# A quarter of a copy in HBM moved from the sync and scalar queues to GpSimd's

## The chip, the cores and the metric

One core of one Trainium2 chip; the metric is the time of one execution on the device, in microseconds, as the median of several executions. The executions that are compared here are of the fast state; one run, the copy within SBUF, also had a slow one, and it is named there. The result was taken on one chip; the experiments ran on two others. Before took 822.3 us on the first and 811.3 to 811.7 us on the others, so every experiment is compared with the runs of before on its own chip.

## The reference

```python
def setup_inputs():
    return {"x": np.random.randn(8192, 8192).astype(np.float32)}

def reference(x):
    return np.fft.ifftshift(x)
```

With both sides even, `ifftshift` swaps the four quadrants crosswise. It is a copy of 268.44 MB with nothing to compute.

## The kernel before

Rows of a quadrant are 4096 floats, 16 KB. A transfer takes every eighth row of one column half: 512 rows, 8 MB. There are 32 such transfers, from HBM to HBM. Those that write the top half of `out` are issued by the sync engine, those that write the bottom half by the scalar engine.

```python
    # STEP = 8, R = C = 8192, hr = hc = 4096
    dims = [[STEP * C, hr // STEP], [1, hc]]
    for c in range(STEP):
        for col in (0, hc):
            for eng, r0, h in ((nc.sync, 0, col), (nc.scalar, hr, hc - col)):
                eng.dma_start(
                    out=bass.AP(out.tensor, out.offset + (r0 + c) * C + h, dims),
                    in_=bass.AP(x.tensor, x.offset + (hr - r0 + c) * C + hc - h, dims),
                )
```

Of the kernel before, what the change touches and what calls it, by code (L numbers as in the profile page):

```python
# [1 line left out]

# [4 lines left out]


STEP = 8  # L10


@with_exitstack
def kernel(
    ctx: ExitStack,
    tc: tile.TileContext,
    x: bass.AP,
    out: bass.AP,
):



    nc = tc.nc

    R, C = x.shape
    hr = R // 2
    hc = C // 2

    dims = [[STEP * C, hr // STEP], [1, hc]]
    for c in range(STEP):  # L30
        for col in (0, hc):
            for eng, r0, h in ((nc.sync, 0, col), (nc.scalar, hr, hc - col)):
                eng.dma_start(
                    out=bass.AP(out.tensor, out.offset + (r0 + c) * C + h, dims),
                    in_=bass.AP(x.tensor, x.offset + (hr - r0 + c) * C + hc - h, dims),
                )


# [1 line left out]
_INS = ['x']  # L40
_OUTS = [((8192, 8192), 'float32')]


def kernel(**inputs):
    import numpy as _np
    import concourse.bacc as _bacc
    import concourse.tile as _tile
    from concourse import mybir as _mybir
    from concourse.bass_utils import run_bass_kernel_spmd as _run

    nc = _bacc.Bacc("TRN2", target_bir_lowering=False, num_devices=1)  # L51
    arrays, args = {}, []
    for name in _INS:
        a = _np.ascontiguousarray(inputs[name])
        if a.dtype.kind in "iu":
            a = a.astype(_np.int64)
        arrays[f"in_{name}_dram"] = a
        args.append(nc.dram_tensor(f"in_{name}_dram", a.shape, _mybir.dt.from_np(a.dtype), kind="ExternalInput").ap())
    for i, (shape, dtype) in enumerate(_OUTS):
        dt = _mybir.dt.from_np(_np.dtype(dtype))  # L60
        args.append(nc.dram_tensor(f"out_{i}_dram", shape, dt, kind="ExternalOutput").ap())
    with _tile.TileContext(nc) as tc:
        kernel(tc, *args)
    r = _run(nc, [arrays], core_ids=[0])
    got = tuple(r.results[0][f"out_{i}_dram"] for i in range(len(_OUTS)))
    return got[0]
```

## Time and profile before

| | before |
|---|---|
| time | 822.26 us (821.98 to 822.82, 6 runs) |
| rate of copying, 20 to 800 us | 328 GB/s |
| bytes read and written in HBM, over the span | 654 GB/s |
| sync queue / scalar queue, share of 16 engines | 50.2% / 49.7% |
| shortest / median / mean packet of 16 KB | 608 / 773 / 801 ns |

The time comes from the result, the rate from a stretch of the timeline, the next rows from the page of the profile, and the last from the trace's record of each packet (a start, a length and a queue). The copied bytes are counted once in "GB/s" and twice, read and written, in the HBM figure. The lines themselves are in the prediction.

### The profile page before, as it was taken

What the parts mean: (1) busy time and instruction counts of PE and PEld (TensorE: products, weight loads), DVE (VectorE), ACT (ScalarE), POOL (GpSimd) and SP (SyncE); (2) the same over time, 40 slices, a digit from 0 to 9 for tenths busy, and PEclk for the clock granted to TensorE, in tenths of its full rate; (3) what the DMA queues carried; (4) which work ended last, traced back from release to release, by engine and by line L of the source; (5) the groups of instructions that cost most, each with busy time, mean ns of one, the idle gap of its engine ahead of it and who ended that gap; (6) DMA issues with size and microseconds to landing.
All of it is one profiled execution on the core that took longest, in us unless ns stands there. A gap on an engine that the chain in (4) does not pass through costs nothing. (4 is left out here: it accounts for less than half of the span.)

```text
span 821.3 us, 77 instructions
## 1 busy us (share of the span) xinstructions
POOL 0.2 (0%) x4
## 2 busy tenths in 40 slices
POOL 0000000000000000000000000000000000000000
DMA  9999999999999999999999999999999999999998
GB/s 304 325 328 333 326 325 330 321 329 330 325 330 330 327 328 333 329 330 330 328 328 327 334 325 330 326 326 328 331 329 330 326 332 326 328 324 333 326 328 298
DMA packets 16896, 268.44 MB, mean 327 GB/s; under 512 B 512, under 2 KB 512, under 8 KB 512
## 3 DMA queue, kind: packets, MB, share of 16 engines
q1 hardware_dynamic: 8448, 134.22, 50.2%
q10 hardware_dynamic: 8448, 134.22, 49.7%
HBM read 268.44 MB, written 268.44 MB: 654 GB/s over the span
## 5 line engine op out<-in xcount | busy, mean ns | idle before, releaser
L51 POOL MEMSET const-bfloat16-1.0<- 128x1 bf16 x1 | 0.1, 103 | 0.0
L51 POOL MEMSET const-uint8-127<- 128x1 uint8 x1 | 0.1, 102 | 0.0
L51 POOL MEMSET const-float32-0.0<- 128x1 f32 x1 | 0.1, 99 | 0.2 <-issue 0.2
L51 POOL MEMSET const-float32-1.0<- 128x1 f32 x1 | 0.1, 99 | 0.0
## 6 DMA issues: line engine op xcount, KB each, us to landing
out_dram<-in_x_dram ACTq DMA_DIRECT2D x16, 8192.0 KB, 204.3
out_dram<-in_x_dram SPq DMA_DIRECT2D x16, 8192.0 KB, 204.1
```

Of the source, the lines that this page charges most:

```text
L51: nc = _bacc.Bacc("TRN2", target_bir_lowering=False, num_devices=1)
```

## The change

The intent is to have a third queue carry a quarter of the rows from the beginning, in the hope that three queues together move more than two. Of every eight neighbouring rows, numbers 6 and 7, counted from 0, go to GpSimd, whose queue the profile calls `software_dynamic`; 0 to 5 stay with sync and scalar, whose queues it calls `hardware_dynamic`.

```diff
-    for c in range(STEP):
+
+    def copy(eng, r0, c, h):
+        eng.dma_start(
+            out=bass.AP(out.tensor, out.offset + (r0 + c) * C + h, dims),
+            in_=bass.AP(x.tensor, x.offset + (hr - r0 + c) * C + hc - h, dims),
+        )
+
+    for c in range(6):
         for col in (0, hc):
-            for eng, r0, h in ((nc.sync, 0, col), (nc.scalar, hr, hc - col)):
-                eng.dma_start(
-                    ... (the same two lines as in copy)
-                )
+            copy(nc.sync, 0, c, col)
+            copy(nc.scalar, hr, c, hc - col)
+        if c < 2:
+            for col in (0, hc):
+                copy(nc.gpsimd, 0, 6 + c, hc - col)
+                copy(nc.gpsimd, hr, 6 + c, col)
```

More of the change, by code (lines that the diff above doesn't have):

```diff
@@ L29 @@
     dims = [[STEP * C, hr // STEP], [1, hc]]
-    for c in range(STEP):
-        for col in (0, hc):
-            for eng, r0, h in ((nc.sync, 0, col), (nc.scalar, hr, hc - col)):
-                eng.dma_start(
-                    out=bass.AP(out.tensor, out.offset + (r0 + c) * C + h, dims),
-                    in_=bass.AP(x.tensor, x.offset + (hr - r0 + c) * C + hc - h, dims),
-                )
+    def copy(eng, r0, c, h):
[4 more added lines that the diff above has]
+    for c in range(6):
+        for col in (0, hc):
+            copy(nc.sync, 0, c, col)
[4 more added lines that the diff above has]
+                copy(nc.gpsimd, hr, 6 + c, col)
 _INS = ['x']
```

## The prediction

> **What bounds the kernel now.** I read the page first: the engines, the slices, the queues, and last the chain. No engine computes anything; the only busy time is 0.2 us of GpSimd's constants. The kernel is a copy from HBM to HBM, so all that counts is what the 16 DMA engines do. From the page:
>
> ```profile
> span 821.3 us, 77 instructions
> ...
> DMA  9999999999999999999999999999999999999998
> GB/s 304 325 328 333 326 325 330 321 329 330 325 330 330 327 328 333 329 330 330 328 328 327 334 325 330 326 326 328 331 329 330 326 332 326 328 324 333 326 328 298
> ...
> q1 hardware_dynamic: 8448, 134.22, 50.2%
> q10 hardware_dynamic: 8448, 134.22, 49.7%
> HBM read 268.44 MB, written 268.44 MB: 654 GB/s over the span
> ```
>
> The DMA row is 9 or more from the first slice to the last but one: there is no idle stretch to fill. The GB/s row hardly moves, 321 to 334 between its ends. The two queues' shares add to 99.9% of sixteen engines' span: together they keep the engines occupied, and each engine works on one packet at a time. 8448 packets a queue are 16 transfers of 512 rows and 16 completion words, so a packet is one row of 16,384 bytes.
>
> Next, whether issue could hold anything up. From the sync engine's waits and the list of issues:
>
> ```profile
> SPq L62 <- DMA out_dram<-in_x_dram: 167.2, 2, 118.8
> SPq L33 <- DMA out_dram<-in_x_dram: 133.8, 12, 50.6
> ...
> out_dram<-in_x_dram ACTq DMA_DIRECT2D x16, 8192.0 KB, 204.3
> out_dram<-in_x_dram SPq DMA_DIRECT2D x16, 8192.0 KB, 204.1
> ```
>
> A transfer lands 204 us after issue, and a queue finishes one about every 51 us (821.3 / 16), so four are in flight on each queue. The 133.8 us that the sync engine waits before issuing are waits for a free place behind three transfers still to be worked off. The 167.2 us is the end of the kernel, when everything is issued and only data is moving. Issue is far ahead of the data.
>
> "DMA busy" alone does not say whether the engines or the memory behind them is the limit. The trace's packet records (a start, a duration and a queue each) do. Of the 16,384 row packets the shortest took 608 ns; about a quarter took 611 ns; the median is 773 and the mean about 800 ns. A pile-up at 611 ns is an engine's own pace with nothing in its way: 16,384 B / 611 ns = 26.8 GB/s. At that pace a kernel of 1024 rows an engine would last 1024 x 0.611 = 626 us. The other 190 us or so are waiting inside packets, for something that all engines share.
>
> Stretches of the timeline tell that it is a steady common ceiling (columns: stretch, its length, GpSimd busy, clock, DMA share, GB/s):
>
> ```profile
> 3.00:5.00 2.00, 0.00 (x0) 1.00 0.92 385
> 5.00:12.00 7.00, 0.00 (x0) 1.00 1.00 351
> 12.00:20.00 8.00, 0.00 (x0) 1.00 1.00 315
> 20.00:420.00 400.00, 0.00 (x0) 1.00 1.00 328
> 420.00:800.00 380.00, 0.00 (x0) 1.00 1.00 328
> ```
>
> 328 GB/s in both long stretches, to the last digit shown. From about 5 to 12 us the packet records show the sixteen engines marching in step, all on the sync queue's rows and then all on the scalar queue's, each packet near 755 ns; later they have drifted apart and durations scatter from 611 to over 1100 ns. The scatter does not move the total. I also sorted the stretch from 20 to 790 us by how many of the engines were on one queue at the instant: the rate is 334 GB/s when all are on the scalar queue, 325 at a half-and-half mixture, 328 when all are on the sync queue. Reads and writes in opposite halves of the matrices or all in the same: it makes under 3%. That is the mark of a bandwidth ceiling, not of two address streams getting in each other's way.
>
> **What the Trainium skill says.** Three places bear on it. "DMA: Bandwidth & Descriptors", section "Issuing engines are not separate DMA queues", says that transfers started by sync, scalar or GpSimd all run on the same 16 engines and interleave, and that issuing from several only saves the sequencers' time. The trace agrees as far as two queues can show it: each takes half of one set of engines. The same page, "SWDGE vs HWDGE vs iDMA", says that GpSimd's transfers have their descriptors written by software into rings in SBUF, and that an engine goes round-robin between its internal queues; no run here shows a GpSimd transfer yet. "HBM Reference", "Specifications (TRN2)", gives about 716 GB/s for a memory stack shared by two cores. The trace's 654 GB/s, read and written together, is 91% of that. It exceeds the 358 GB/s that the page calls effective per core, so one core alone is not held to that share. I take 654 of 716 as a ceiling nearly reached; an estimate from the page's figure of the least time is 536.9 MB / 716 GB/s = 750 us[...].
>
> **The change part by part.** The program's order shows that bytes, rows and transfer shapes stay: 32 transfers of 512 rows of 16 KB. Four of sync's 16 and four of scalar's go to GpSimd, which issues eight with no wait between them; sync and scalar keep 12 each, the last eight of each with the same kind of wait as before.
>
> - Removed: 4 issues of some 42 us each from each of the two hardware queues. They lay beside data movement and were not on the path: worth 0.
> - Moved: a quarter of the packets, 8 x 512 = 4096 rows, to a third ring. Under the ceiling a packet costs its bytes whoever issued it: 67.1 MB / 328 GB/s = 205 us before and after: 0.
> - Added at the start: GpSimd's descriptors are made in software and may come a microsecond or so later than the others' first packets (an estimate; the skill's first-byte figures differ by less). Sync and scalar fill the engines meanwhile: 0.
> - Added at the end: if the three rings take turns, GpSimd moves at a third of 328 = 109 GB/s and ends its 67.1 MB at about 614 us. By then sync and scalar have moved as much each and hold 33.6 MB each, which last 67.1 MB / 328 GB/s = 205 us more. Sum 819 us, plus some 2 us before the first packet: 821 us. GpSimd is not last, so its completion handling is hidden.
> - Gain from the order in memory: three streams instead of two, with the same stride and sizes. The sort above bounds what a mixture is worth, 325 to 334: some -1% to +2%, with no reason for a sign.
>
> Sum: 821 us, against 822.3.
>
> **The rivals.**
>
> *A. The third stream raises the ceiling.* For it: for about two microseconds at the start, when only the sync queue is on, packets take about 625 ns, which is some 420 GB/s; so the memory can at least briefly take more than 328. The first-slices rates (385, 351) carry the same hint. Against it: from 20 us on, nothing in which queue is active moves the rate. If three rings took away a quarter of the 190 us of waiting, the time would be about 775 us; a tenth would give 803.
>
> *B. Software-made packets are dearer.* If a GpSimd row were cut into smaller pieces, or its descriptor fetched from the ring late, that row would take longer. For it: the skill says the rings lie in SBUF and that two of the engines are usually slower in traces, with such rings as its best guess. Every transfer is split evenly over 16 engines, so a slow pair would end last. Against it: an engine waits on average 800 - 611 = 190 ns of each packet, so an extra 100 ns on a quarter of the packets can disappear into time that is waiting anyway. If it did not disappear, 256 GpSimd rows an engine x 100 ns = 26 us: 848 us.
>
> *C. GpSimd becomes the last.* If its ring gets a smaller turn, or only few of its transfers fit, it is alone at the end. With a fifth of the rate while three are on, it would have 67.1 - 50.3 = 16.8 MB left when the others end. At the full rate of 328 that costs nothing; at half that rate, 51 us more: about 870 us. Against it: at the end of the trace of before the scalar queue is alone for about 2 us, with packets at 666 to 743 ns, no slower than in company. One ring can drive all engines; a software ring is untested.
>
> **Range and chances.** The centre is the ceiling: 821 us. The mixture's effect of -1% to +2% in rate gives about 806 to 829, widened for a mild form of A or B on either side: 804 to 840 should hold it 8 times in 10. Faster by over 2% (below 806) needs A, for which only the first microseconds speak: 0.13. Slower by over 2% (above 839) needs B or C beyond the slack: 0.13. Within 2%: 0.74.
>
> **What would show it right or wrong.** In the changed profile there should be a third queue with 67.11 MB and some 4096 packets over the completion words, and each queue's share of the engines' time in proportion to its bytes, about a quarter for GpSimd; the three still adding to about 100%. The GB/s row should stay near 328 while three queues are on and after GpSimd's end, near 614 us. The prediction is wrong if the row steps up or down at that moment (A or B); if GpSimd's queue has many more packets than its rows, or a share well above a quarter (B); or if the last slices fall while it is alone (C). Since the kernel before is steady to 0.1%, even a shift of 1% would be real, but inside what I call the same.

## The result, and the profile after

The changed kernel took 822.45 us (821.44 to 823.29, 6 runs) against 822.26 us. The ratio is 1.0001, with a 95% interval of 0.9988 to 1.0014: the same, and to within a seventh of a per cent. Ratios here are the mean time of one kernel's fast runs over that of the other's of the same rounds, so they are not quite the ratio of the medians quoted.

From the page of the changed kernel, the slices, the queues (packets, MB, share of 16 engines' span) and the issues (count, KB each, median us to landing):

```profile
span 819.7 us, 81 instructions
...
GB/s 305 330 323 329 331 325 332 328 330 329 322 333 328 328 330 325 328 330 332 330 326 336 330 328 330 329 327 329 332 327 333 324 333 326 324 333 329 329 332 295
...
q1 hardware_dynamic: 6336, 100.66, 37.4%
q10 hardware_dynamic: 6336, 100.66, 37.0%
q0 software_dynamic: 4224, 67.11, 25.3%
HBM read 268.44 MB, written 268.44 MB: 655 GB/s over the span
...
L32 POOL DMA_DIRECT2D out_dram<-in_x_dram x8 | 5.0, 631 | 0.8 <-PEq L70 0.8
...
out_dram<-in_x_dram SPq DMA_DIRECT2D x12, 8192.0 KB, 270.1
out_dram<-in_x_dram ACTq DMA_DIRECT2D x12, 8192.0 KB, 267.6
out_dram<-in_x_dram POOLq DMA_DIRECT2D x8, 8192.0 KB, 346.7
```

The third queue is there with a quarter of the bytes and a quarter of the engines' time (25.3%), and the other two have given up just that: 50.2 to 37.4 and 49.7 to 37.0. The three add to 99.7%, where the two added to 99.9. GpSimd issued all eight in 5 us. A transfer of sync's now takes 270 us from issue to landing in place of 204, because three rings share what two shared; that costs nothing, as the last landing is what counts.

The decisive view is the rate in stretches, because GpSimd's queue runs dry on the way: by the packet records its last packet ended 614.0 us after the kernel's first, 616 us into the span. Columns: stretch, its length, GpSimd busy, clock, DMA share, GB/s.

```profile
20.00:200.00 180.00, 0.00 (x0) 1.00 1.00 329
200.00:420.00 220.00, 0.00 (x0) 1.00 1.00 329
420.00:600.00 180.00, 0.00 (x0) 1.00 1.00 329
600.00:700.00 100.00, 0.00 (x0) 1.00 1.00 329
700.00:800.00 100.00, 0.00 (x0) 1.00 1.00 330
```

Three queues until 616 us, two after, and the rate doesn't notice: 329, 329, 330. Before that, from 20 to 600 us, the records count 3886 packets of GpSimd's, 3883 of sync's and 3872 of scalar's: equal turns. GpSimd's packets averaged 810 ns, sync's 798, scalar's 790. That software makes these 2% is not shown: the shortest is 608 ns on all three queues.

### The profile page after: what moved, and what is told of

It reads as the page before. It is cut to its first block, busy times and chain, and to the rows that moved or that the text cites. A ratio compares the mean times of both kernels' runs of the same rounds, so it can differ in the third digit from the quotient of the medians.

```text
span 819.7 us, 81 instructions
## 1 busy us (share of the span) xinstructions
POOL 5.2 (1%) x12
## 3 DMA queue, kind: packets, MB, share of 16 engines
q1 hardware_dynamic: 6336, 100.66, 37.4%
q0 software_dynamic: 4224, 67.11, 25.3%
## 5 line engine op out<-in xcount | busy, mean ns | idle before, releaser
L32 POOL DMA_DIRECT2D out_dram<-in_x_dram x8 | 5.0, 631 | 0.8 <-PEq L70 0.8
```

The source lines that it names most:

```text
L32: eng.dma_start(out=bass.AP(out.tensor, out.offset + (r0 + c) * C + h, dims), in_=bass.AP(x.tensor, x.offset + (hr - r0 + c) * C + hc - h, ...
```

## The experiments

The theory: some 330 GB/s of copying is a ceiling that all engines run into together, and neither the number nor the kind of the queues matters to it. The rivals: more queues do overlap better or worse; software-made packets are dearer and the small share hid it; the ceiling depends on the order of addresses; or 800 ns is simply an engine's own pace.

**All on GpSimd.** If software packets had a cost hidden by their being a quarter, four times as many show it.

```diff
-            for eng, r0, h in ((nc.sync, 0, col), (nc.scalar, hr, hc - col)):
+            for eng, r0, h in ((nc.gpsimd, 0, col), (nc.gpsimd, hr, hc - col)):
```

> All 32 transfers on GpSimd's queue, none on sync's and scalar's. Theory (a ceiling in the memory, about 328 GB/s of copying, common to all engines; who issues does not matter): 822 us within 1%, one queue with a share near 100%, packets of 611 ns at least and about 800 on average. Rival B (software-made packets are dearer, and the slack hid it while they were a quarter): with four times as many, 840 us or more, shortest packets longer than 611 ns, or two engines that end late. Rival C (a software ring alone cannot keep the engines full): GB/s clearly under 328, 870 us or more.

812.15 us against 811.29: ratio 1.0012 (0.9995 to 1.0028). The page and GpSimd's waits:

```profile
q0 software_dynamic: 16896, 268.44, 99.5%
HBM read 268.44 MB, written 268.44 MB: 662 GB/s over the span
...
POOL out_dram L33 <- DMA out_dram<-in_x_dram: 589.0, 24, 25.6
```

One software queue fills sixteen engines to 99.5%. The shortest packet is 608 ns as on the hardware queues, and the mean 787 ns is that of the next run, with all on sync. No two engines end late: sixteen packets are still under way 0.8 us before the last one ends. GpSimd spends 589 us waiting to issue its later transfers, each until an earlier one has landed: it too is ahead of the data. Rivals B and C fall for rows of 16 KB.

**All on sync.**

```diff
-            for eng, r0, h in ((nc.sync, 0, col), (nc.scalar, hr, hc - col)):
+            for eng, r0, h in ((nc.sync, 0, col), (nc.sync, hr, hc - col)):
```

> All 32 transfers on sync's hardware queue. Theory: 822 us within 1%, as with two or three queues. Rival A in its modest form (more queues overlap better): one queue should be worse than two, 830 us or more. A second reading of the first microseconds (one queue alone ran at some 420 GB/s, so one stream is what the memory likes): clearly under 806 us.

811.31 us against 811.29: ratio 1.0001 (0.9986 to 1.0016).

```profile
q1 hardware_dynamic: 16896, 268.44, 99.5%
```

One, two or three queues are the same. This also disposes of the only thing that spoke for rival A, the fast start when only the sync queue was on. Here only the sync queue is on throughout, and the packet records show the same course: 614 to 617 ns in the second and third microsecond of data, 743 in the fifth, about 787 from 20 us on. The start is fast because it is the start, not because one queue is alone. Why the ceiling lets more through for three microseconds isn't settled.

**The order of addresses.** Neighbouring rows in a transfer in place of every eighth.

```diff
-    dims = [[STEP * C, hr // STEP], [1, hc]]
+    dims = [[C, hr // STEP], [1, hc]]
...
-   (r0 + c) * C + h          (hr - r0 + c) * C + hc - h
+   (r0 + c * hr // STEP) * C + h    (hr - r0 + c * hr // STEP) * C + hc - h
```

> The kernel before with transfers of 512 neighbouring rows instead of every eighth row: same bytes, rows, queues and engines, other order of addresses (row pitch 32 KB in place of 256 KB, engines 1 MB apart in place of 8 MB). If the ceiling is a plain bandwidth that does not care for the order: 822 us within 1%. If the ceiling depends on the pattern of addresses, and the third queue changed nothing only because it kept the pattern: a difference of over 2%, either way.

811.56 us against 811.29: ratio 1.0007 (0.9984 to 1.0030). A third order (neighbouring rows to neighbouring engines; each transfer starts at row c * hr // STEP, as in the run before) was run later as a control for the runs with 14 engines:

```diff
-    dims = [[STEP * C, hr // STEP], [1, hc]]
+    dims = [[C, 16], [16 * C, hr // STEP // 16], [1, hc]]
```

> Control for the runs with fewer engines: the same order of rows (neighbouring rows to neighbouring engines) on all 16. Theory (the ceiling does not care for the order): 811 to 812 us, as before's on this chip, within 1%. If this order itself is slower, part of the 5.7% of the run with 14 engines was its order.

813.95 us against 811.63: ratio 1.0012 (0.9978 to 1.0046). So three orders of addresses agree to 0.5% at worst. The stride of every eighth row is itself worth nothing measurable on these chips. All three orders have strides that are powers of two, 32 KB and up. The nearest thing to another is in the runs with 14 engines below, where an engine's own rows are 448 KB apart and the rate, while all fourteen work, is the same.

**Half the engines.** A slowest dimension of 8 entries is meant to put a transfer on 8 engines (rows in the order of the control above).

```diff
-    dims = [[STEP * C, hr // STEP], [1, hc]]
+    dims = [[C, 8], [8 * C, hr // STEP // 8], [1, hc]]
```

> The same copy on 8 of the 16 DMA engines (slowest dimension of 8 entries), 2048 rows an engine. Theory (packets wait for the memory, which 16 engines overload): with half the demand the packets all run near the engines' own 611 ns, 8 x 26.8 = 214 GB/s, 2048 x 0.611 = 1251 us plus some 4. Rival (800 ns is the engines' own pace for copies in HBM, with a chance spread): packets keep a mean near 800 ns, 1638 us.

1249.64 us, where the theory said 1251 plus some 4 and the rival 1638. The packets on its page, and a long stretch of the run:

```profile
DMA packets 16640, 268.44 MB, mean 215 GB/s; under 512 B 256, under 2 KB 256, under 8 KB 256
...
20.00:420.00 400.00, 0.00 (x0) 1.00 0.50 216
```

The 256 packets under 512 bytes are completion words, 8 for each of 32 transfers where before had 16, and half the engines' time is used (0.50): eight engines it is. The packets no longer scatter: mean 611.3 ns, 99.9% of them at 608 to 612. So 611 ns is what an engine by itself takes for a packet, and the other 190 ns of before are spent because sixteen run at once.

**Fourteen engines.** If the ceiling is common, 14 engines should reach it as well as 16.

```diff
+    E = 14; n = hr // STEP // E     # 36; the 8 rows over go as a transfer of their own
-    dims = [[STEP * C, hr // STEP], [1, hc]]
+    dims = [[C, E], [E * C, n], [1, hc]]      # and [[C, 8], [1, hc]] for the rest
```

> The copy of before on 14 of the 16 engines (a few left-over rows on engines 0 to 7). At their own pace they would need at most 1184 x 0.611 = 723 us. Theory (one ceiling common to all engines, which 14 still reach: 14 x 26.8 = 375 GB/s of pace against some 330): the same time as with 16, within 1.5%, and shorter packets, about 14/16 of the mean. Rival (each engine has a share of its own in the ceiling, by its port): 16/14 of the time, some 14% longer.

858.77 us, ratio 1.0574 (1.0547 to 1.0601): between the two expectations. I blamed the left-over rows, which load eight of the engines and put short transfers among the long ones, and moved them once to the start:

```diff
+    for eng, r0, h in quads:
+        copy(eng, r0, h, 0, 8, 1)             # 8 rows of each quadrant, once
+    for m in (36, 36, 36, 36, 37, 37, 37, 37):  # then only transfers of 14 x m rows
```

> 14 engines again, with the left-over rows moved once at the start, so that every engine has 1170 or so rows and no short transfer sits among the long ones. Theory (ceiling common to all engines; the 5.7% before was eight engines left alone at the end with 215 GB/s, and short transfers that took places in flight): GB/s near 332 all along, within 2.5% of before, the rest being engines that do not end together. Rival (14 engines have less of the ceiling): GB/s clearly lower from the start, 5% or more.

866.29 us, ratio 1.0679 (1.0661 to 1.0697). It got worse, so my reason was wrong. The stretches show what it is instead:

```profile
20.00:220.00 200.00, 0.00 (x0) 1.00 0.88 330
220.00:470.00 250.00, 0.00 (x0) 1.00 0.87 331
470.00:770.00 300.00, 0.00 (x0) 1.00 0.82 315
775.00:860.00 85.00, 0.00 (x0) 1.00 0.50 216
```

While all fourteen work (0.88 of sixteen is 14), the rate is 330 to 331, the same as with sixteen: the ceiling is common, and the rival's 14% is not there. But the fourteen do not share it evenly. At the end eight of them are alone for 85 us at 216 GB/s, the pace of the run with eight engines. From 475 to 775 us there are spells with only eight packets under way, some 40 us in all: the other six then have nothing in flight. The loss is in the sharing, not in the total.

The packet records carry no engine number, but they show the sharing all the same. A packet mostly starts 3 or 4 ns before an earlier one ends, and so the packets of one engine can be strung together wherever just one fits. From 20 to 220 us this gives 71 strings of 20 packets or more. In 36 of them the mean packet is 611 to 621 ns, in 35 it is 749 to 804 ns, and in none is it between. The same for the kernel before, with sixteen engines and from 20 to 800 us, gives 287 strings, all of them with a mean from 771 to 833 ns. So some of the fourteen engines run almost undisturbed and the others carry all the waiting, while sixteen engines share it. An estimate: if six ran at 611 ns and eight shared the remaining 331 - 6 x 26.8 = 170 GB/s, the eight would be at 771 ns; the slow strings average 777. The six would end their 1170 rows at 715 us and the eight at 863 us, close to the span of 862.7. (In the run the eight are alone for less than these 148 us at the end, because the six were idle before.) It is not that each eight has a limit of its own near 170, since eight alone reach 216. Why six are spared isn't shown.

**Reads alone, writes alone** (wrong results): the same rows of `x` into SBUF with three tiles in turn, or all of `out` from one tile of zeros. In outline:

```diff
-   eng.dma_start(out=<rows of out>, in_=<rows of x>)
+   eng.dma_start(out=<tile in SBUF>, in_=<rows of x>)     # reads alone, one 8 MB block out at the end
+   eng.dma_start(out=<rows of out>, in_=<tile in SBUF>)   # writes alone, in the other kernel
```

> Wrong result on purpose: x is only read, into SBUF, same rows in the same order; out gets one block of 8 MB. If the ceiling is on reads and writes of HBM together (some 655 to 662 GB/s): reads alone come up against the engines' pace first, 16 x 26.8 = 429 GB/s, 626 us and about 20 for the last block: some 650 us. If reads have a ceiling of their own at 328 to 331 GB/s: 820 us or more.

> Wrong result on purpose: out is only written, from one tile of zeros in SBUF; x is not read. If the ceiling is on reads and writes together: the engines' pace, 429 GB/s, 626 us and about 20 for the fill before: some 650 us. If writes have a ceiling of their own at 328 to 331 GB/s: 820 us or more.

654.51 us and 651.02 us, at 0.81 and 0.80 of before. The stretch from 220 to 420 us of each:

```profile
220.00:420.00 200.00, 0.00 (x0) 1.00 1.01 428
```

```profile
220.00:420.00 200.00, 0.00 (x0) 0.00 (x0) 1.00 1.01 427
```

Either direction alone runs at the engines' own pace (16 x 26.8 = 429), with packets of 611 to 622 ns nearly throughout. Neither reads nor writes are limited to 330; what meets the ceiling is both at once.

**From SBUF to SBUF** (wrong result): is the ceiling at HBM, or in something the engines share whatever they copy? In outline:

```diff
-   eng.dma_start(out=<rows of out>, in_=<rows of x>)
+   eng.dma_start(out=<one of four tiles>, in_=<one tile of zeros>)    # 64 of 4 MB
```

> Wrong result on purpose: the same 268 MB from SBUF to SBUF, HBM hardly touched. If the ceiling of some 331 GB/s of copying lies on the way to HBM or in it: the engines' own pace, about 429 GB/s, 626 us and 20 to 25 for the fill before and the last block. If it lies in the engines or in what they share for any copy (reading and writing 662 GB/s together): 811 us and more, packets of 16 KB and up slowed in the same way.

994.46 us in the fast execution (the other, 1023.12, slow): neither expectation. Its rate was 285 GB/s in a stretch from 20 to 420 us, and packets of 32 KB took 1832 ns in the median against 1213 at the least, so this path has a limit of its own, a lower one. It is no measure of the other, and where the copy's ceiling sits, in the memory or in what lies between it and the engines, stays open.

**GpSimd's rows in small pieces.** The changed kernel, with every row of GpSimd's cut into pieces of 1 KB (even pieces in one transfer, odd in another).

```diff
+        w = 256 if eng is nc.gpsimd else hc
+        for odd in range(2 if w < hc else 1):
+            d = dims if w == hc else [dims[0], [2 * w, hc // (2 * w)], [1, w]]
             eng.dma_start(... + odd * w, d)
```

> The changed kernel, but GpSimd's quarter of the rows goes in pieces of 1 KB (16 packets where there was one), so software writes 16 times as many descriptors. Theory (dearer packets on a quarter disappear in the waiting as long as an engine's own paces add to less than the total: 768 rows x 0.611 = 469 us, which leaves 340 us for 4096 pieces, 83 ns each): same time within 2% if a piece takes less than 83 ns unobstructed, as 611/16 = 38 ns and a little overhead would. Rival B: software descriptors cannot be made or fetched that fast: 840 us or more, with GpSimd's queue last.

820.09 us, ratio 1.0092 (1.0076 to 1.0109). It is within the 2% and not for the reason given. The queues, and the stretches while all three were on and after; the profiled execution was the slowest of its five, 828.45 us:

```profile
q1 hardware_dynamic: 6336, 100.66, 35.5%
q10 hardware_dynamic: 6336, 100.66, 34.4%
q0 software_dynamic: 16640, 67.11, 29.1%
```

```profile
20.00:220.00 200.00, 2.04 (x1) 1.00 1.00 333
220.00:420.00 200.00, 4.07 (x2) 1.00 1.00 333
420.00:680.00 260.00, 4.08 (x2) 1.00 1.01 332
690.00:820.00 130.00, 14.27 (x7) 1.00 0.99 308
```

While three queues were on, the rate was 333. That is a mild test of slack, since undisturbed the four packets that now make up a row take 4 x 159 = 636 ns, 25 more than one of 16 KB. What moved is the order of ending. GpSimd's 16,384 packets are of 4 KB, four pieces each; the hardware queues' are of 16 KB, and a turn goes by packets: from 20 to 220 us the records count 1836 of GpSimd's, 1807 of sync's and 1800 of scalar's. By bytes that is a share of about 4/36 = 11%, not a third. The hardware queues ended 691 us into the span with their 201.3 MB, when GpSimd had moved 27 MB (12%). Its other 40 MB came alone, at 308 GB/s, with packets of 210 ns on average where the undisturbed ones took 159: less than 333, though the engines were in full use (0.99). This is rival C, at a small size. The last stretch is also the first sign that small pieces alone don't reach the ceiling of whole rows.

**All rows in pieces of 512 bytes**, on the two queues of before: does the slack hide dearer packets when all are dearer?

```diff
-    dims = [[STEP * C, hr // STEP], [1, hc]]
+    dims = [[STEP * C, hr // STEP], [256, 16], [1, 128]]     # even pieces; odd ones from + 128
```

> The kernel before in pieces of 512 bytes, on the two hardware queues: what a dearer packet costs when all are dear. The 1 KB pieces went at 159 ns for four, 40 ns each, so 2 ns over 611/16 = 38; at the same overhead 512 bytes take 19 + 2 = 21 ns, 16 KB 680 ns, which is still under the 785 or so that the ceiling gives: theory says within 2% of before. Rival B (small packets eat the slack): if a piece takes over 25 ns, the engines' pace takes over, and the time is 1024 x 32 x that: 30 ns would make 983 us.

882.19 us, ratio 1.0886 (1.0853 to 1.0918); the theory's "within 2%" was wrong. The stretch from 20 to 220 us:

```profile
20.00:220.00 200.00, 0.00 (x0) 1.00 1.10 305
```

The median record of a piece is 27 ns, not 21, and 32 x 27 = 864 ns a row, over 1024 rows 885 us, is near the span of 880.3. It is tempting to conclude that the engines now go at their own pace. The records speak against it. They overlap by some 3.5 ns (hence a share above 1), so 27 ns isn't the time from one piece to the next. From 4 to 5 us, when every piece took 27 ns, an engine did one every 23.6 ns and the sixteen 348 GB/s; at that pace a row takes 755 ns, less than the 785 that the ceiling gives. From 20 us on it was one piece every 26.6 to 26.9 ns, at 305 to 308 GB/s. So undisturbed pieces would have fitted into the slack, and the time still rose by 8.9%: small pieces make the whole slower in another way. Whether the common ceiling is lower for them, as the 308 GB/s of GpSimd's last pieces suggest, or the making of 32 times as many pieces holds the engines up, isn't shown.

No version ran faster than the kernel before.

## Why the prediction was right

- *A ceiling common to all engines, reached already.* Shown. Eight engines wait for nothing (611 ns), fourteen have the same total as sixteen, and reads or writes alone don't meet it. The direct evidence for the change is that the rate is 329 with three queues and 329 to 330 after GpSimd's end. What the Trainium skill says in "DMA: Bandwidth & Descriptors", "Issuing engines are not separate DMA queues", holds here: one queue made 811.31 us against 811.29 for two, three made 822.45 against 822.26 on the other chip. That the ceiling is the memory's bandwidth, 654 of 716 GB/s, as the prediction takes it, is not shown: no run says where it sits.
- *It doesn't care for the order of addresses.* Argued from the sort by queue; shown by three orders within 0.5%, all with strides of powers of two. The prediction allowed -1% to +2% for it and needed none.
- *Moved: 205 us before and after.* Right: 25.3% of the engines' time of 819.7 us is 207.
- *GpSimd ends at about 614 us and is not last.* Measured 614.0 after the first packet; that the last digit fits is luck. The working supposed turns by equal packets, which held because all three queues' packets were rows of 16 KB. The run with 1 KB pieces shows that it needn't: there the packets were 4 KB, the turn a quarter, and GpSimd was last.
- *Removed issues and the start are worth nothing.* Right. GpSimd's first packet came 3.8 us after sync's and 0.6 us after scalar's, where "a microsecond or so" was forecast. The first-byte figures meant there are those of "DMA: Bandwidth & Descriptors", "Specifications": about 1 us for GpSimd's path, 0.6 for the others'. Each alone, GpSimd's first packet started at 2.7 us and sync's at 2.1: 0.6 us apart, where the page has 0.4.
- *The sum of 821 us* is a span, set beside a time of 822.3 us. The spans were 821.3 before and 819.7 to 821.5 after, so it makes no difference here.
- *Rival A* rested on the first microseconds, which are as fast with one queue for good. *Rival B* was answered with slack: 190 ns of waiting in which a dearer row disappears. The runs answer it more simply. GpSimd's rows were not dearer: at their shortest they took 608 ns like the others, and with all of them on GpSimd the ratio was 1.0012. In the changed kernel they exceeded the others' mean by 12 to 19 ns. So the 26 us for a B that does not disappear were never put to the test, and the slack itself is not shown: pieces of 512 bytes would have fitted into it at their undisturbed pace, and cost 8.9%. The slow pair of engines that B leans on is in "DMA: Bandwidth & Descriptors", "Latency and other measured facts"; no run here shows one.
- *Rival C* has a loose reading against it: "alone for about 2 us, with packets at 666 to 743 ns". In the records the scalar queue is alone for 3.3 us, and its packets then take 611 to 1114 ns. The better evidence came later, with one queue alone throughout.

## What to carry to other kernels

When packets last longer on average than the shortest of them while all engines are busy, look for what they share: here more queues added nothing to a common ceiling. Don't count on the waiting to hide dearer packets: a small share of them cost nothing in rate here (333 GB/s), but all rows in small pieces cost 8.9%, although the pieces alone would have been fast enough. Queues took turns by packets, so the queue with smaller packets got a smaller share and ended last; compare packet sizes before trusting an even split. And leaving engines out doesn't only remove their pace: here it made the rest share unevenly.

## What the Trainium skill lacked or had wrong

- "HBM Reference", "Specifications (TRN2)": it has no figure for a copy within HBM, where reads and writes meet. The runs show 328 to 333 GB/s of copying in rows of 16 KB, 654 to 663 read and written over the span, against 427 to 428 for either alone; and chips differ by 1.3% in it, while an engine's 611 ns a row is the same on all three. "DMA: Bandwidth & Descriptors", "Latency and other measured facts", does have a figure for copies between HBM tensors in rows of 16 KiB, 214 GB/s per direction as the full rate and less at row pitches of 512 KiB and up; the runs here, in rows of the same size, are well above it.
- "DMA: Bandwidth & Descriptors", "Queues, rings and completion order": it gives 9 to 17 descriptors as typical of the packet by which queues take turns. In the records here one turn of a hardware queue was one row of 16 KB, and one of GpSimd's was one row of 16 KB or four pieces of 1 KB. (Four pieces are the 4096 bytes that the same page, in "SWDGE vs HWDGE vs iDMA", gives as preferred.) The share follows: 12% for 4 KB packets beside two queues of 16 KB.
- The same page, "Why small descriptors are slow (HBM only)": three cycles of overhead a packet make 512/32 + 3 = 19 cycles, an estimate of 22 ns at the page's 850 MHz. That is near the 23.6 ns from piece to piece in the first microseconds; it lacks that a whole copy in such pieces goes slower, 26.6 to 26.9 ns from piece to piece and 305 to 308 GB/s.
- The same page, "Where 436 GB/s comes from": it names 435 GB/s as binding for transfers within SBUF. A copy from one tile to others within the same partitions ran at 285.
- No page has what a copy within HBM on fewer than sixteen engines does: of fourteen, some ran at 611 to 621 ns a row and the others at 749 to 804, and eight were left alone at 216 GB/s for 85 us.
